# Attention's exponentials kept in the scores' bank, with a written beginning and a turned end, in a two-layer hybrid encoder

## The chip, the cores and the metric

The kernel runs on one core of one Trainium2 chip. The metric is the device time of one execution in microseconds (us), the median of several runs. The engines are called by the profile's names: PE is TensorE (matmuls; PEld its weight loads), DVE is VectorE, ACT is ScalarE, POOL is GpSimd, SP is SyncE, which issues most transfers. A bank is one of the eight parts of PSUM, 512 fp32 columns wide, which matmuls write. GpSimd does not use banks in this kernel.

## The reference

Everything is fp32; 512 tokens of 1024 channels go through two layers, each with an MLP behind it:

```python
for i in range(2):
    h = rms_norm(x, g[0])
    m = parallel_conv_mla(h, ...) if i == 0 else conformer_conv(h, ...)
    x = x + rms_norm(m, g[1])
    x = x + rms_norm(squared_relu_mlp(rms_norm(x, g[2])), g[3])

def parallel_conv_mla(h, ...):             # layer 0
    gate_b, gate_c, xs, q_lat, kv_lat, k_rope = split(h @ w_in)
    y_a = gate_b * depthwise_conv(gate_c * xs, width 3)
    q = (rms_norm(q_lat) @ w_uq) per head; k_nope, v = (rms_norm(kv_lat) @ w_ukv) per head
    y_b = softmax((q . k) * scale) @ v     # 8 heads, rotary part of 32, 512 x 512 scores
    return concatenate([y_a, y_b]) @ w_out

def conformer_conv(h, ...):                # layer 1
    u = a * sigmoid(g)                     # a, g = split(h @ w_pw1 + b)
    u = silu(layer_norm(depthwise_conv(u, width 31) + b))
    return u @ w_pw2 + b

def squared_relu_mlp(h, w1, w2):           # hidden 4096
    return square(relu(h @ w1)) @ w2
```

## The kernel before

Channels lie on the 128 partitions, tokens on the free axis: x is eight tiles of 128 x 512. Each fp32 product is made of three matmuls on values split into a high and a low part (`mm`, lines 246 to 248: high by high, high by low, low by high). A weight strip of 128 x 1024 is loaded by SP, rounded to its high part by ACT (L223), and its low part is subtracted by POOL (L224); two raw buffers and eight pairs of split ones turn over. `accum` hands out banks: three named S, two pj; one more is named o and two mi.

The order of work. Most instructions are put in order by a planner that simulates the engines; inside a `manual_schedule` the named engines keep the order in which the code writes them. `strip` calls come from a queue that `take` keeps some strips ahead.

- *Beginning* (L554 to L618). x comes in eight tiles; DVE scales each by a gain (L572), ACT rounds it (L230), DVE subtracts the low part (L233). The squares of x are summed (`Sum`, L358 and L333), summed over channels by matmuls (L368), `rstd` (L384) finds the root on DVE, `spread` (L433) brings it to all partitions, and R0 is 1 over the root mean square. The projections of the raw x (`linear` with win's strips) are multiplied by R0 afterwards (L608), so their banks are held until R0 is there. Five strips make the latents, the sixth the rotary key, twelve the short convolution.
- *Attention* (`project`, `attend`, in the order of `ATT`). For each head and block of 128 queries: scores into a bank S (L759), maximum (L761), exponential with its sum from the bank into an SBUF tile pr (L764), reciprocal, scaling of pr in place (L767; on POOL for head 7's first three blocks, else on DVE), transposes into a bank mi (L770), split into the pair PT (ACT L230, DVE L236), and after two blocks the product with V into o.
- *Two halves and a program.* After attention the tokens are cut into halves A and B. `M2` is a list of steps: up and down are the MLP's two products, pw1 and pw2 the conformer's, norm, join and finish the chains of small steps between. While a chain runs, `hold` and `pace` pull following steps of the other half to fill TensorE (`step` stops at a step of the same half). The depthwise convolution runs on DVE in pieces: `fill` adds a credit in us for each step of TensorE's, and taps are issued as long as the credit pays for them (0.395 us each with two convolutions under way, 0.525 alone). Half A is 272 wide in layer 0, B 240; in layer 1 both are 256.
- *End* (`turn`, `end`). For half B the last product is turned, tokens on partitions. `end_step` adds the last group (L1029), squares (L1031), multiplies by the gain on POOL (L1032), makes the root (L1035 with `rstd`), scales and adds the residual (L1051) and stores (L1055). Its second block's second half of columns goes in two pieces.

Of the kernel before, what the change touches and what calls it, by code (L numbers as in the profile page):

```python
# [9 lines left out]
F32 = mybir.dt.float32  # L10
# [22 lines left out]
PAD = 16  # L33
M0 = [('wout', 'A'), ('join', 'A', 0, 1), ('wout', 'B')]
M1 = []
M2 = [('up', 'A', 0, 0, 0, 8), ('join', 'B', 0, 1), ('down', 'A', 0, 0, 0, 8), ('up', 'A', 0, 1, 0, 8), ('down', 'A', 0, 1, 0, 8), ('up', 'A', 0, 2, 0, 8), ('down', 'A', 0, 2, 0, 8), ('up', 'A', 0, 3, 0, 8), ('down', 'A', 0, 3, 0, 8), ('join', 'A', 0, 3), ('up', 'B', 0, 0, 0, 8), ('down', 'B', 0, 0, 0, 4), ('pw1', 'A', 0, 8), ('down', 'B', 0, 0, 4, 8), ('up', 'B', 0, 1, 0, 8), ('down', 'B', 0, 1, 0, 8), ('up', 'B', 0, 2, 0, 2), ('norm', 'A'), ('up', 'B', 0, 2, 2, 8), ('down', 'B', 0, 2, 0, 8), ('pw2', 'A', 0, 8), ('join', 'A', 1, 1), ('up', 'B', 0, 3, 0, 8), ('down', 'B', 0, 3, 0, 8), ('join', 'B', 0, 3), ('up', 'A', 1, 0, 0, 8), ('down', 'A', 1, 0, 0, 4), ('pw1', 'B', 0, 8), ('down', 'A', 1, 0, 4, 8), ('up', 'A', 1, 1, 0, 8), ('down', 'A', 1, 1, 0, 8), ('up', 'A', 1, 2, 0, 6), ('norm', 'B'), ('up', 'A', 1, 2, 6, 8), ('down', 'A', 1, 2, 0, 8), ('up', 'A', 1, 3, 0, 4), ('pw2', 'B', 0, 8), ('join', 'B', 1, 1), ('up', 'A', 1, 3, 4, 8), ('down', 'A', 1, 3, 0, 8), ('up', 'B', 1, 0, 0, 8), ('turn', 'B', 1, 0, 0, 6), ('finish', 'A'), ('turn', 'B', 1, 0, 6, 8), ('up', 'B', 1, 1, 0, 8), ('residual', 'B'), ('turn', 'B', 1, 1, 0, 8), ('up', 'B', 1, 2, 0, 8), ('turn', 'B', 1, 2, 0, 8), ('up', 'B', 1, 3, 0, 8), ('end', 'B', 1, 3)]
# [6 lines left out]
START = ['x', (128,), 'x', (256, 512, 768), 'x', 'x', 'x', 'x', 'x', 'x', ()]  # L43
ADD0 = 0
LAG = 4
MULT_POOL = (0, 0, 0, 0, 0, 0, 0, 3)
W0 = True
WHOLE = (True,) * 5
WL = True
# [81 lines left out]
def trunk(ctx: ExitStack, tc: tile.TileContext, a, out: bass.AP, out_b: bass.AP):  # L131
# [435 lines left out]
    s0 = Sum(NC, FULL, nc.gpsimd if ADD0 else nc.vector, whole=W0)

    def split_x(j):
        load_x(xs[j], j)  # L570
        t, (hi, lo) = scratch(T), (h.t[:, :T] for h in hs[j])
        nc.vector.tensor_scalar(out=t, in0=xs[j].t, scalar1=col(gains(0, 0) + j), scalar2=None, op0=ALU.mult)  # L572
        settle()
        split((hi, lo), t, nc.vector, late=late)
        if j >= LAG:
            s0.square(xs[j - LAG].t)

    win, j = [], 0
    for what in START:
        if what == "x":  # L580
            split_x(j)
            j += 1
        else:
            win.append(strip(a["win"][len(win)], cuts=what))
    nc.sync.dma_start(kst, a["consts"])
    nc.sync.dma_start(vec[:, V_QN:], a["vecs"][:, V_QN:])
    settle()
    for j in range(NC - LAG, NC):
        s0.square(xs[j].t)
        settle()  # L590
# [299 lines left out]
    def up_step(tok, h, layer, g, m):  # L890
# [124 lines left out]
    def end_step(tok, h, layer, g):  # L1015
# [19 lines left out]
        def root(b):  # L1035
            s = misc()[:, :1]
            p = parts[b]
            if len(p) == 3:
                nc.vector.scalar_tensor_tensor(
                    out=s, in0=p[0], scalar=p[1], in1=p[2], op0=ALU.add, op1=ALU.add  # L1040
                )
            else:
                nc.vector.tensor_tensor(out=s, in0=p[0], in1=p[1], op=ALU.add)
            return rstd(s, D, tuple(f[:, b : b + 1] for f in f12))

        def leave(b, r, n):
            w = T // n
            for f in range(2):
                for i in range(n):
                    m, x = (t[:, i * w : i * w + w] for t in turned[b, f][1:])  # L1050
                    nc.vector.scalar_tensor_tensor(  # L1051
                        out=x, in0=m, scalar=r, in1=x, op0=ALU.mult, op1=ALU.add
                    )
                    q = nc.scalar if i % 2 else nc.sync
                    q.dma_start(out_b[b * P : (b + 1) * P, f * T + i * w : f * T + i * w + w], x)  # L1055
# [204 lines left out]
```

## Time and profile before

| | |
|---|---|
| median of 3 runs | 1172.47 us (1171.79 to 1172.93) |
| profiled execution | 1173.47 us |
| its span, first to last instruction | 1171.7 us |
| busy: PE, DVE, ACT, POOL | 1134.6, 649.2, 661.5, 846.0 us |
| mean granted clock of TensorE | 0.993 |

The profile is one execution. An engine's idle time counts only where that engine sets the pace. A busy PE is not PE at its peak, because ends of pipelined matmuls are modelled; the number of matmuls in a stretch tells more. In a row, "[1.47 <-DVE ...]" is idle time before it and who ended it.

### The profile page before, as it was taken

Reading aid. Unit: us, or ns where it says so; the run is one execution under the profiler, and the core shown is the slowest. Engines: PE = TensorE matmul, PEld = TensorE weight load, DVE = VectorE, ACT = ScalarE, POOL = GpSimd, SP = SyncE. Lnnn points to the kernel's source line nnn. Section 1 sums busy time; section 2 is a strip of 40 time slices with the busy share of each in tenths; the row PEclk is TensorE's granted clock in tenths of the full one; section 3 lists DMA queues with packets and bytes.
Section 4 is the critical chain, followed back from the end, with each engine's and each line's share of the span. In section 5 each row is a group of like instructions: output and inputs, shape, how many; then the busy total and the mean of one; then the engine's idle time right before and its main releaser. Section 6 shows DMA issues by size and latency. Waiting matters only on the chain.

```text
span 1171.7 us, 22121 instructions
## 1 busy us (share of the span) xinstructions
PE 1134.6 (97%) x8492; PEld 1081.3 (92%) x8492; DVE 649.2 (55%) x1693; ACT 661.5 (56%) x1211; POOL 846.0 (72%) x408
## 2 busy tenths in 40 slices
PE   7999989999999999999999999999999999999996
PEld 5778778999999999999999999999999999898895
DVE  5672699455432222669996364589995254131134
ACT  5431677456744445744655686745566776455451
POOL 5663563148878778688898578789787878779881
PEclk9999999999999999999999899999999999999999
DMA  6421332027545555545565355556555545565530
GB/s 222 154 90 30 106 100 72 1 92 235 201 161 182 178 180 169 174 163 181 180 216 187 122 196 181 179 171 207 169 195 178 180 163 180 165 231 182 179 108 36
DMA packets 55257, 184.47 MB, mean 157 GB/s; under 512 B 6384, under 2 KB 10352, under 8 KB 55152
## 3 DMA queue, kind: packets, MB, share of 16 engines
q1 hardware_dynamic: 54576, 182.02, 46.9%
q8 instruction: 66, 1.08, 0.4%
q10 hardware_dynamic: 576, 1.05, 0.3%
q14 instruction: 39, 0.32, 0.1%
HBM read 180.94 MB, written 2.10 MB: 156 GB/s over the span
## 4 chain that ended last, share of the span: by engine, by line
PE 85%; DVE 6%; ACT 3%; DMA 3%; POOL 1%; issue 1%; SPq 0%; DVEq 0%; ACTq 0%; POOLq 0%
PE S L246 20%; PE S L247 19%; PE S L248 19%; PE pj L246 5%; PE pj L247 5%; PE pj L248 5%; PE pj L990 4%; PE S L990 4%; DMA raw<-in_win 2%; POOL wlo L224 1%; ACT whi L223 1%; DVE pr L767 1%; DMA raw<-in_w 1%; PE mi L433 1%; PE mi L770 1%
## 5 line engine op out<-in xcount | busy, mean ns | idle before, releaser
L224 POOL TENSOR_TENSOR wlo<-raw,whi 128x1024 fp32r<-128x1024 f32 (+2 forms) x347 | 802.0, 2327 | 263.2 <-ACT whi L223 243.6
L223 ACT ACTIVATE whi<-raw 128x1024 fp32r<-128x1024 f32 (+2 forms) x347 | 356.6, 1033 | 368.7 <-PE S L247 173.3
L246 PE MATMUL S<-h,whi 128*128 128x256 f32 (+3 forms) x1208 | 347.7, 291 | 5.0 <-ACT h L230 2.9
L247 PE MATMUL S<-h,whi 128*128 128x256 f32 (+3 forms) x1208 | 349.0, 290 | 0.0
L248 PE MATMUL S<-h,wlo 128*128 128x256 f32 (+3 forms) x1208 | 348.7, 289 | 0.0
L246 PEld LDWEIGHTS S<-h,whi 128*128 128x128 f32 x1208 | 229.0, 191 | 10.1 <-ACT h L230 3.4
L247 PEld LDWEIGHTS S<-h,whi 128*128 128x128 f32 x1208 | 230.5, 191 | 3.5 <-issue 0.2
L248 PEld LDWEIGHTS S<-h,wlo 128*128 128x128 f32 x1208 | 230.5, 191 | 3.3 <-POOL wlo L224 0.3
L832 DVE SCALAR_TENSOR_TENSOR pj<-u,taps,pj 128x256 f32<-128x256 f32 x464 | 192.6, 484 | 1.3
L246 PE MATMUL S<-hid,whi 128*128 128x256 f32 (+2 forms) x664 | 185.3, 281 | 1.4 <-DVE acc L333 1.2
L248 PE MATMUL S<-hid,wlo 128*128 128x256 f32 (+2 forms) x664 | 186.5, 282 | 0.0
L247 PE MATMUL S<-hid,whi 128*128 128x256 f32 (+2 forms) x664 | 186.3, 281 | 0.0
L246 PEld LDWEIGHTS S<-hid,whi 128*128 128x128 f32 x664 | 124.8, 189 | 2.5 <-DVE acc L333 1.8
L248 PEld LDWEIGHTS S<-hid,wlo 128*128 128x128 f32 x664 | 125.3, 189 | 0.0
L247 PEld LDWEIGHTS S<-hid,whi 128*128 128x128 f32 x664 | 125.3, 189 | 0.0
L246 PE MATMUL pj<-h,whi 128*128 128x256 f32 (+3 forms) x344 | 105.5, 307 | 9.5 <-ACT h L230 7.6
L248 PE MATMUL pj<-h,wlo 128*128 128x256 f32 (+3 forms) x344 | 105.3, 306 | 0.3 <-POOL wlo L224 0.3
L247 PE MATMUL pj<-h,whi 128*128 128x256 f32 (+3 forms) x344 | 105.3, 306 | 0.0
L246 PEld LDWEIGHTS pj<-h,whi 128*128 128x128 f32 x344 | 65.5, 191 | 12.4 <-ACT h L230 7.6
L236 DVE TENSOR_TENSOR hid<-S,hid 128x256 fp32r<-128x256 f32 (+2 forms) x102 | 42.9, 420 | 52.7 <-ACT hid L230 52.2
L247 PEld LDWEIGHTS pj<-h,whi 128*128 128x128 f32 x344 | 65.5, 190 | 3.4 <-DVE h L233 1.1
L248 PEld LDWEIGHTS pj<-h,wlo 128*128 128x128 f32 x344 | 65.6, 191 | 3.1 <-POOL wlo L224 0.7
(267 smaller groups left out, 1740.2 us busy)
## 6 DMA issues: line engine op xcount, KB each, us to landing
raw<-in_w SPq DMA_DIRECT2D x224, 512.0 KB, 3.3
raw<-in_pw SPq DMA_DIRECT2D x48, 512.0 KB, 3.3
raw<-in_w2t SPq DMA_DIRECT2D x32, 512.0 KB, 3.3
raw<-in_win SPq DMA_DIRECT2D x16, 512.0 KB, 3.3
x<-in_xT SPq DMA_DIRECT2D x16, 256.0 KB, 4.4
raw<-in_wout SPq DMA_DIRECT2D x8, 512.0 KB, 3.3
raw<-in_wq SPq DMA_DIRECT2D x8, 192.0 KB, 2.4
out<-x SPq DMA_DIRECT2D x8, 128.0 KB, 3.5
```

Source lines behind the costliest of these rows:

```text
L223: nc.scalar.activation(h, r, AF.Copy)
L224: nc.gpsimd.tensor_tensor(out=lo[:, c0:c1], in0=r, in1=h.bitcast(F32), op=ALU.subtract)
L236: eng.tensor_tensor(out=lo, in0=src, in1=hi.bitcast(F32), op=ALU.subtract)
L246: nc.tensor.matmul(acc, sh, mh, start=i == 0, stop=False)
L247: nc.tensor.matmul(acc, sh, ml, start=False, stop=False)
L248: nc.tensor.matmul(acc, sl, mh, start=False, stop=i == n - 1)
L433: nc.tensor.matmul(o[:, sl], r[:, b : b + 1].to_broadcast([bw, P]), ident[:bw, :bw], start=True, stop=True,)
L767: eng.tensor_scalar(out=pr_, in0=pr_, scalar1=sm, scalar2=None, op0=ALU.mult)
L770: nc.tensor.transpose(tp[:, kb * P : (kb + 1) * P], pr_[:, kb * P : (kb + 1) * P], ident)
L832: nc.vector.scalar_tensor_tensor(out=dst, in0=src, scalar=wk, in1=acc, op0=ALU.mult, op1=ALU.add)
L990: nc.tensor.matmul(acc, x, w, start=start, stop=stop)
```

## The change

Five edits go together.

1. The beginning is written out for PE, DVE and ACT. PE starts with twelve matmuls on a zeroed tile (`busy`) and does ten more after the first product. The first two strips take each x as it comes (`bit`), strips 3 and 4 follow; the sums of squares and the root stand between them. Banks of the first four products are pj, S, pj, S.
2. Attention: on 23 of the 32 blocks the exponential is written back into the bank S, and DVE scales from there into pr. On nine blocks (head 1 to 5: block 1; heads 6 and 7: blocks 0 and 2) it goes to pr and POOL scales it.
3. M2: norm A comes two up steps later, and pw2 A two up steps of the next group later.
4. The credits of up and down steps are scaled by the half's width over 256.
5. The end: the gain product is made by DVE into the bank, squares go to bank o, the last piece has a bank of its own, the mean and the first sums are made ahead, and the root is a shorter chain. The gain's load moves from ACT's queue, where it stood behind M0, to SP at the first turn step.

```diff
-... ('up', 'B', 0, 2, 0, 2), ('norm', 'A'), ('up', 'B', 0, 2, 2, 8), ('down', 'B', 0, 2, 0, 8), ('pw2', 'A', 0, 8), ('join', 'A', 1, 1), ('up', 'B', 0, 3, 0, 8), ...
+... ('up', 'B', 0, 2, 0, 4), ('norm', 'A'), ('up', 'B', 0, 2, 4, 8), ('down', 'B', 0, 2, 0, 8), ('up', 'B', 0, 3, 0, 2), ('pw2', 'A', 0, 8), ('join', 'A', 1, 1), ('up', 'B', 0, 3, 2, 8), ...
...
-MULT_POOL = (0, 0, 0, 0, 0, 0, 0, 3)
+MULT_POOL = [(h, 1) for h in range(1, 6)] + [(h, b) for h in (6, 7) for b in (0, 2)]
...
+    E = mybir.EngineType
+    with tc.manual_schedule(engines={E.PE, E.DVE, E.Activation}):
+        idle, bank = tmp("tq", F32R), ps("S")
+        nc.vector.memset(idle.bitcast(F32), 0.0)
+        def busy(n):
+            for _ in range(n):
+                nc.tensor.matmul(bank, idle[:, :P], idle, start=True, stop=True)
+        accs = []
+        def bit(i, k):
+            if len(accs) == i:
+                accs.append(ps(("pj", "S")[i % 2]))
+            (wh, wl), (xh, xl), kk = win[i], hs[k], slice(k * P, k * P + P)
+            x_h, x_l = xh.t[:, :T], xl.t[:, :T]
+            nc.tensor.matmul(accs[i], wh[:, kk], x_h, start=k == 0, stop=False)
+            nc.tensor.matmul(accs[i], wl[:, kk], x_h, start=False, stop=False)
+            nc.tensor.matmul(accs[i], wh[:, kk], x_l, start=False, stop=k == NC - 1)
+        busy(12)
+        win, scaled, sq = [], [], {}
+        total = ps("o")
+        def scale_x(j):
+            load_x(xs[j], j)
+            t = misc()
+            nc.vector.tensor_scalar(out=t, in0=xs[j].t, scalar1=col(gains(0, 0) + j), scalar2=None, op0=ALU.mult)
+            nc.scalar.activation(hs[j][0].t[:, :T], t, AF.Copy)
+            scaled.append(t)
+        def rest_x(j):
+            hi, lo = (h.t[:, :T] for h in hs[j])
+            nc.vector.tensor_tensor(out=lo, in0=scaled[j], in1=hi.bitcast(F32), op=ALU.subtract)
+        def square_x(j):
+            sq[j] = tmp("ycat") if j else total
+            nc.scalar.activation(sq[j], xs[j].t, AF.Square)
+        def add_x(j):
+            dst = tmp("ycat") if j == NC - 1 else total
+            nc.vector.tensor_tensor(out=dst, in0=total, in1=sq[j], op=ALU.add)
+            return dst
+        scale_x(0)
+        win.append(strip(a["win"][0], cuts=(128,)))
+        rest_x(0)
+        bit(0, 0)
+        busy(10)
+        scale_x(1)
+        win.append(strip(a["win"][1], cuts=(256, 512, 768)))
+        bit(1, 0)
+        for j in range(2, NC + 1):
+            if j < NC:
+                scale_x(j)
+            if j >= 5:
+                square_x(j - 5)
+            rest_x(j - 1)
+            bit(0, j - 1)
+            bit(1, j - 1)
+        win.append(strip(a["win"][2]))
+        nc.sync.dma_start(kst, a["consts"])
+        nc.sync.dma_start(vec[:, V_QN:], a["vecs"][:, V_QN:])
+        for j in range(1, NC):
+            if j + 3 < NC:
+                square_x(j + 3)
+            if j == 4:
+                win.append(strip(a["win"][3]))
+            last = add_x(j)
+        for k in range(NC):
+            bit(2, k)
+        win.append(strip(a["win"][4]))
+        s0 = Sum(NC, FULL)
+        s0.parts = [last]
+        root = rstd(s0.done(STARTS), D, inverse=inv0)[:, :NB]
+        for k in range(NC - 2):
+            bit(3, k)
+        nc.scalar.activation(R0, spread(root), AF.Copy)
+        for k in range(NC - 2, NC):
+            bit(3, k)
+    scope["turn"] = 3
...
-            acc = linear(win[m0 + j] if m0 + j < len(win) else strip(a["win"][m0 + j]), hs)
+            acc = accs[m0 + j] if m0 + j < len(accs) else linear(win[m0 + j], hs)
...
-            nc.scalar.activation(pr_, S, AF.Exp, bias=mx, scale=SCALE, accum_out=sm)
+            on_pool = (h, b) in MULT_POOL
+            e = pr_ if on_pool else S
+            nc.scalar.activation(e, S, AF.Exp, bias=mx, scale=SCALE, accum_out=sm)
             nc.vector.reciprocal(sm, sm)
-            eng = nc.gpsimd if b < MULT_POOL[h] else nc.vector
-            eng.tensor_scalar(out=pr_, in0=pr_, scalar1=sm, scalar2=None, op0=ALU.mult)
+            eng = nc.gpsimd if on_pool else nc.vector
+            eng.tensor_scalar(out=pr_, in0=e, scalar1=sm, scalar2=None, op0=ALU.mult)
...
-        fill(FILL["up"])
+        fill(FILL["up"] * seg.w / 256)
-        fill(FILL["sum" if last else "down" if g else "first"])
+        fill(FILL["sum" if last else "down" if g else "first"] * seg_of(h, layer).w / 256)
...
-            turned["gain"] = gtok
+            nc.sync.dma_start(gtok, a["gain"].to_broadcast([P, D]))
...
+        scaled = {b: [] for b in range(2)}
+        def piece(b, f, cols, acc=None):
+            bank, m, x = turned[b, f]
+            acc = bank[:, cols] if acc is None else acc
+            m, x, g = m[:, cols], x[:, cols], gtok[:, f * T + cols.start : f * T + cols.stop]
             nc.vector.tensor_tensor(out=m, in0=acc, in1=m, op=ALU.add)
             sm = small(1)
+            nc.scalar.activation(ps("o")[:, : acc.shape[-1]], m, AF.Square, accum_out=sm)
+            nc.vector.tensor_tensor(out=acc, in0=m, in1=g, op=ALU.mult)
             parts[b].append(sm)
+            scaled[b].append((acc, x, f * T + cols.start))
+        def near(b):
+            fd, v = small(1), small(1)
+            nc.vector.tensor_scalar(
+                out=fd, in0=f12[1][:, b : b + 1], scalar1=1.0 / D, scalar2=None, op0=ALU.mult
+            )
+            v0 = parts[b][0]
+            for p in parts[b][1:]:
+                nc.vector.tensor_tensor(out=v0, in0=v0, in1=p, op=ALU.add)
+            nc.vector.tensor_scalar(out=v, in0=v0, scalar1=fd, scalar2=EPS, op0=ALU.mult, op1=ALU.add)
+            return fd, v
+        def root(b, fd, v):
+            nc.vector.scalar_tensor_tensor(
+                out=v, in0=parts[b][-1], scalar=fd, in1=v, op0=ALU.mult, op1=ALU.add
+            )
+            r, y, q, out = (small(1) for _ in range(4))
+            nc.vector.tensor_scalar(
+                out=r.bitcast(I32), in0=v.bitcast(I32), scalar1=-0.5, scalar2=float(0x5F3759DF),
+                op0=ALU.mult, op1=ALU.add,
+            )
+            nc.vector.scalar_tensor_tensor(out=y, in0=r, scalar=v, in1=r, op0=ALU.mult, op1=ALU.mult)
+            nc.vector.tensor_scalar(out=q, in0=y, scalar1=0.375, scalar2=-1.25, op0=ALU.mult, op1=ALU.add)
+            nc.vector.tensor_scalar(out=q, in0=q, scalar1=y, scalar2=1.875, op0=ALU.mult, op1=ALU.add)
+            nc.vector.tensor_tensor(out=r, in0=q, in1=r, op=ALU.mult)
+            nc.vector.scalar_tensor_tensor(out=y, in0=r, scalar=v, in1=r, op0=ALU.mult, op1=ALU.mult)
+            nc.vector.tensor_scalar(out=q, in0=y, scalar1=-0.5, scalar2=1.5, op0=ALU.mult, op1=ALU.add)
+            nc.vector.scalar_tensor_tensor(
+                out=out, in0=q, scalar=r, in1=f12[0][:, b : b + 1], op0=ALU.mult, op1=ALU.mult
+            )
+            return out
+        def leave(b, r):
+            for i, (m, x, c) in enumerate(scaled[b]):
+                nc.vector.scalar_tensor_tensor(out=x, in0=m, scalar=r, in1=x, op0=ALU.mult, op1=ALU.add)
+                q = nc.scalar if i % 2 else nc.sync
+                q.dma_start(out_b[b * P : (b + 1) * P, c : c + x.shape[-1]], x)
+        def rest(f, cols, acc=None):
+            acc = turned[1, f][0][:, cols] if acc is None else acc
+            n = f * T + cols.start
             for k in range(NC):
+                issue([turn_mm(acc, h, ws[k], k, 1, slice(0, cols.stop - cols.start), n)])
         for f in range(2):
             piece(0, f, slice(0, T))
+            if f == 0:
+                fd, v = near(0)
         rest(0, slice(0, T))
+        leave(0, root(0, fd, v))
         piece(1, 0, slice(0, T))
         for i in range(2):
             cols = slice(i * T // 2, (i + 1) * T // 2)
+            acc = (ps("S") if i else turned[1, 1][0])[:, : T // 2]
+            rest(1, cols, acc)
+            if i:
+                fd, v = near(1)
+            piece(1, 1, cols, acc)
+        leave(1, root(1, fd, v))
...
-    nc.scalar.dma_start(gtok, a["gain"].to_broadcast([P, D]))
```

## Rows read from the trace of the kernel before

**Rows 1.** The page: busy time of each engine.
```profile
PE 1134.6 (97%) x8492; PEld 1081.3 (92%) x8492; DVE 649.2 (55%) x1693; ACT 661.5 (56%) x1211; POOL 846.0 (72%) x408
```

**Rows 2.** TensorE's waits, whole span: waiter, releaser, total us, times, longest.
```profile
PE o L247 <- DVE s L762: 2.5, 3, 1.3
...
PE pj L990 <- ACT pj L1031: 1.1, 1, 1.1
...
PE S L246 <- ACT pr L764: 0.5, 1, 0.5
...
PE mi L662 <- DVE ycat L660: 0.3, 1, 0.3
```

**Rows 3.** Windows: length, busy us (x instructions), granted clock, DMA share, GB/s.
```profile
7.60:12.40 4.80, 4.79 (x10) 3.11 (x11) 3.85 (x6) 3.78 (x8) 3.93 (x4) 1.00 1.01 353
12.40:17.20 4.80, 4.80 (x22) 3.86 (x21) 4.70 (x9) 3.90 (x7) 0.96 (x2) 1.00 0.82 296
...
140.00:200.00 60.00, 55.05 (x351) 47.67 (x350) 58.23 (x130) 44.75 (x96) 33.08 (x19) 1.00 0.30 101
200.00:216.00 16.00, 15.79 (x117) 14.57 (x116) 12.54 (x36) 10.60 (x26) 4.67 (x3) 1.00 0.01 2
...
648.60:654.20 5.60, 5.60 (x28) 5.60 (x28) 4.32 (x12) 4.60 (x12) 0.00 (x0) 0.50 0.00 0
654.40:660.00 5.60, 5.60 (x49) 5.60 (x48) 0.00 (x0) 3.18 (x6) 2.04 (x1) 1.00 0.00 0
```

**Rows 4.** Timeline of the beginning: start, us, engine, line, operation, count.
```profile
0.73 0.42 ACTq L1133 DMA_DIRECT2D gtok<-in_gain  x1
...
7.61 0.80 PE L246 MATMUL pj<-h,whi 128*128 128x512 f32 x1 [7.61 <-ACT h L230]
...
11.56 0.63 PE L248 MATMUL S<-h,wlo 128*128 128x512 f32 x1
...
23.04 1.06 ACT L223 ACTIVATE whi<-raw 128x1024 fp32r<-128x1024 f32 x1 [1.04 <-DMA raw<-in_win]
...
24.18 2.40 POOL L224 TENSOR_TENSOR wlo<-raw,whi 128x1024 fp32r<-128x1024 f32 x1 [1.98 <-ACT whi L223]
...
42.04 0.50 PE L246 MATMUL pj<-h,whi 128*128 128x512 f32 x1 [1.47 <-DVE ycat L608]
...
57.22 0.69 DVE L630 TENSOR_SCALAR ycat<-mi 128x512 f32<-128x512 f32 x1
```

**Rows 5.** Attention, by line: duration ns min/median/max, first and last start.
```profile
L767 DVE TENSOR_SCALAR pr<-pr,s x29: 469/486/3669, 138.4 to 215.8; 128x512 f32<-128x512 f32 x29
...
L767 POOL TENSOR_SCALAR pr<-pr,s x3: 1563/1563/1572, 208.0 to 211.9; 128x512 f32<-128x512 f32 x3
...
L236 DVE TENSOR_TENSOR pt<-mi,pt x32: 661/680/693, 142.9 to 225.2; 128x512 fp32r<-128x512 f32 x32
...
L761 DVE TENSOR_REDUCE s<-S x32: 669/678/692, 135.5 to 210.1; 128x1 f32<-128x512 f32 x32
...
L764 ACT ACTIVATE pr<-S,s x32: 667/688/692, 137.4 to 214.8; 128x512 f32<-128x512 f32 x32
```

**Rows 6.** TensorE's waits from 630 to 660 us, around norm A.
```profile
PE mi L433 <- DVE s L419: 2.3, 1, 2.3
PE S L246 <- ACT h L230: 1.9, 1, 1.9
PE mi L368 <- DVE acc L333: 0.5, 1, 0.5
```

**Rows 7.** Timeline of the end.
```profile
1162.30 0.28 PE L990 MATMUL pj<-whi,hid 128*128 128x256 f32 x1
...
1163.14 0.39 ACT L1031 ACTIVATE pj<-u 128x256 f32<-128x256 f32 x1 [3.75 <-DVE u L1029]
...
1163.68 0.79 DVE L1039 SCALAR_TENSOR_TENSOR mi<-s,s,s 128x1 f32<-128x1 f32 x1 [0.58 <-ACT pj L1031]
...
1167.22 1.67 DVE L1051 SCALAR_TENSOR_TENSOR u<-u,s,u 128x256 f32<-128x256 f32 x4
```

More of the change, by code (lines that the diff above doesn't have):

```diff
@@ L35 @@
 M1 = []
-M2 = [('up', 'A', 0, 0, 0, 8), ('join', 'B', 0, 1), ('down', 'A', 0, 0, 0, 8), ('up', 'A', 0, 1, 0, 8), ('down', 'A', 0, 1, 0, 8), ('up', 'A', 0, 2, 0, 8), ('down', 'A', 0, 2, 0, 8), ('up', 'A', 0, 3, 0, 8), ('down', 'A', 0, 3, 0, 8), ('join', 'A', 0, 3), ('up', 'B', 0, 0, 0, 8), ('down', 'B', 0, 0, 0, 4), ('pw1', 'A', 0, 8), ('down', 'B', 0, 0, 4, 8), ('up', 'B', 0, 1, 0, 8), ('down', 'B', 0, 1, 0, 8), ('up', 'B', 0, 2, 0, 2), ('norm', 'A'), ('up', 'B', 0, 2, 2, 8), ('down', 'B', 0, 2, 0, 8), ('pw2', 'A', 0, 8), ('join', 'A', 1, 1), ('up', 'B', 0, 3, 0, 8), ('down', 'B', 0, 3, 0, 8), ('join', 'B', 0, 3), ('up', 'A', 1, 0, 0, 8), ('down', 'A', 1, 0, 0, 4), ('pw1', 'B', 0, 8), ('down', 'A', 1, 0, 4, 8), ('up', 'A', 1, 1, 0, 8), ('down', 'A', 1, 1, 0, 8), ('up', 'A', 1, 2, 0, 6), ('norm', 'B'), ('up', 'A', 1, 2, 6, 8), ('down', 'A', 1, 2, 0, 8), ('up', 'A', 1, 3, 0, 4), ('pw2', 'B', 0, 8), ('join', 'B', 1, 1), ('up', 'A', 1, 3, 4, 8), ('down', 'A', 1, 3, 0, 8), ('up', 'B', 1, 0, 0, 8), ('turn', 'B', 1, 0, 0, 6), ('finish', 'A'), ('turn', 'B', 1, 0, 6, 8), ('up', 'B', 1, 1, 0, 8), ('residual', 'B'), ('turn', 'B', 1, 1, 0, 8), ('up', 'B', 1, 2, 0, 8), ('turn', 'B', 1, 2, 0, 8), ('up', 'B', 1, 3, 0, 8), ('end', 'B', 1, 3)]
@@ new lines @@
+M2 = [('up', 'A', 0, 0, 0, 8), ('join', 'B', 0, 1), ('down', 'A', 0, 0, 0, 8), ('up', 'A', 0, 1, 0, 8), ('down', 'A', 0, 1, 0, 8), ('up', 'A', 0, 2, 0, 8), ('down', 'A', 0, 2, 0, 8), ('up', 'A', 0, 3, 0, 8), ('down', 'A', 0, 3, 0, 8), ('join', 'A', 0, 3), ('up', 'B', 0, 0, 0, 8), ('down', 'B', 0, 0, 0, 4), ('pw1', 'A', 0, 8), ('down', 'B', 0, 0, 4, 8), ('up', 'B', 0, 1, 0, 8), ('down', 'B', 0, 1, 0, 8), ('up', 'B', 0, 2, 0, 4), ('norm', 'A'), ('up', 'B', 0, 2, 4, 8), ('down', 'B', 0, 2, 0, 8), ('up', 'B', 0, 3, 0, 2), ('pw2', 'A', 0, 8), ('join', 'A', 1, 1), ('up', 'B', 0, 3, 2, 8), ('down', 'B', 0, 3, 0, 8), ('join', 'B', 0, 3), ('up', 'A', 1, 0, 0, 8), ('down', 'A', 1, 0, 0, 4), ('pw1', 'B', 0, 8), ('down', 'A', 1, 0, 4, 8), ('up', 'A', 1, 1, 0, 8), ('down', 'A', 1, 1, 0, 8), ('up', 'A', 1, 2, 0, 6), ('norm', 'B'), ('up', 'A', 1, 2, 6, 8), ('down', 'A', 1, 2, 0, 8), ('up', 'A', 1, 3, 0, 4), ('pw2', 'B', 0, 8), ('join', 'B', 1, 1), ('up', 'A', 1, 3, 4, 8), ('down', 'A', 1, 3, 0, 8), ('up', 'B', 1, 0, 0, 8), ('turn', 'B', 1, 0, 0, 6), ('finish', 'A'), ('turn', 'B', 1, 0, 6, 8), ('up', 'B', 1, 1, 0, 8), ('residual', 'B'), ('turn', 'B', 1, 1, 0, 8), ('up', 'B', 1, 2, 0, 8), ('turn', 'B', 1, 2, 0, 8), ('up', 'B', 1, 3, 0, 8), ('end', 'B', 1, 3)]
@@ L42 @@
 FILL = {'up': 2.3, 'down': 2.3, 'first': 2.6, 'sum': 1.8, 'pw1': 4.8, 'pw2': 2.3}
-START = ['x', (128,), 'x', (256, 512, 768), 'x', 'x', 'x', 'x', 'x', 'x', ()]
-ADD0 = 0
-LAG = 4
-MULT_POOL = (0, 0, 0, 0, 0, 0, 0, 3)
+MULT_POOL = [(h, 1) for h in range(1, 6)] + [(h, b) for h in (6, 7) for b in (0, 2)]
 W0 = True
@@ L565, in trunk @@
     hs = [hpair() for _ in range(NC)]
[L567 to L590, printed above, removed]
     def spread_sb(r):
@@ L599, in trunk @@
     inv0 = cp.tile([P, len(STARTS)], F32, name="inv0")
-    nc.scalar.activation(R0, spread(rstd(s0.done(STARTS), D, inverse=inv0)[:, :NB]), AF.Copy)
+    E = mybir.EngineType
[69 more added lines that the diff above has]
+            bit(3, k)
@@ L1024, in end_step @@
         parts = {b: [] for b in range(2)}
-        def piece(b, f, cols):
-            acc, m, _ = turned[b, f]
-            acc, m, g = acc[:, cols], m[:, cols], turned["gain"][:, f * T + cols.start : f * T + cols.stop]
+        scaled = {b: [] for b in range(2)}
[3 more added lines that the diff above has]
+            m, x, g = m[:, cols], x[:, cols], gtok[:, f * T + cols.start : f * T + cols.stop]
             nc.vector.tensor_tensor(out=m, in0=acc, in1=m, op=ALU.add)
@@ L1030, in piece @@
             sm = small(1)
-            nc.scalar.activation(acc, m, AF.Square, accum_out=sm)
-            nc.gpsimd.tensor_tensor(out=m, in0=m, in1=g, op=ALU.mult)
+            nc.scalar.activation(ps("o")[:, : acc.shape[-1]], m, AF.Square, accum_out=sm)
+            nc.vector.tensor_tensor(out=acc, in0=m, in1=g, op=ALU.mult)
             parts[b].append(sm)
[L1035 to L1055, printed above, removed]
@@ L1057, in rest @@
-        def rest(f, cols):
+            scaled[b].append((acc, x, f * T + cols.start))
[9 more added lines that the diff above has]
+            return fd, v
@@ L1058, in rest @@
+        def leave(b, r):
[6 more added lines that the diff above has]
+            n = f * T + cols.start
             for k in range(NC):
-                issue([turn_mm(turned[1, f][0], h, ws[k], k, 1, cols, f * T)])
+                issue([turn_mm(acc, h, ws[k], k, 1, slice(0, cols.stop - cols.start), n)])
@@ L1061, in end_step @@
         for f in range(2):
             piece(0, f, slice(0, T))
+            if f == 0:
+                fd, v = near(0)
         rest(0, slice(0, T))
-        r = root(0)
-        leave(0, r, 1)
+        leave(0, root(0, fd, v))
         piece(1, 0, slice(0, T))
@@ L1068, in end_step @@
             cols = slice(i * T // 2, (i + 1) * T // 2)
-            rest(1, cols)
-            piece(1, 1, cols)
-        leave(1, root(1), 2)
+            acc = (ps("S") if i else turned[1, 1][0])[:, : T // 2]
[4 more added lines that the diff above has]
+        leave(1, root(1, fd, v))
     def run(program, in_order=True):
```

## The prediction

> **What bounds the kernel now.** I read the page first: of a span of 1171.7 us the matmuls fill 1134.6 [rows 1]. So TensorE sets the time, and a change can only win where TensorE waits, runs at the lower clock, or has not begun or has already ended. The table of TensorE's waits says where that is, and the timeline around each place says why. There are four places, and this change touches all four.
>
> *Beginning.* The first matmul starts at 7.61. Up to 12.4 ten matmuls of 512 columns take 4.8 us, then 22 take the same time [rows 3, 4]. The granted clock is shown as 1.00 for both, but 0.48 against 0.22 us is the 1.2 GHz level against the 2.4 GHz level; the engine had done nothing before. At 42.04 TensorE waits 1.47 us because all five score and projection banks hold products that wait for R0 [rows 4].
>
> *Attention.* From 140 to 200 us VectorE is busy 58.2 of 60 us and TensorE is idle 4.95 [rows 3]; the waits named are for VectorE [rows 2]. The reader should see one odd row: the 29 scalings on VectorE have a median of 486 ns and a maximum of 3669 ns [rows 5]. I laid the long ones (eight of the 29) beside GpSimd's instructions: each overlaps one of GpSimd's subtractions and ends when it ends. The 29 take 24.1 us in all, 14.1 at the median, so 10.0 us of VectorE is waiting. The scaling reads and writes SBUF. VectorE's low-part subtraction reads a bank, ran 32 times in the same stretch, and never left 661 to 693 ns [rows 5].
>
> *Norm A.* TensorE waits 0.5, 2.3 and 1.9 us at three steps of the layer norm [rows 6], and just after the granted clock is 0.50, the 1.2 GHz level: 28 matmuls in 5.6 us, against 49 later [rows 3]. That cost 2.4 us, and 0.2 more in the half microsecond before.
>
> *End.* TensorE waits 1.1 us for a square that is written into its bank [rows 2]; after its last matmul, through at 1162.6 [rows 7], 9.1 us follow.
>
> **The change part by part.**
>
> *Beginning.* Taken away: the lower level (11 matmuls at 0.43, 2.4 us), since 12 idle matmuls run from about 1.4 us; and the wait for a bank (1.47), since the root is now asked for in the middle of strip 3, some 7 us earlier. The gain vector (512 KB, issued on ScalarE's queue at 0.73 [rows 4]) no longer loads beside the first x: at the 353 GB/s of that stretch [rows 3] that is up to 1.5 us earlier, or nothing if the planner puts it first on SP. Added: waits of the written order. Two strips need 6 matmuls for each x, 1.32 us, so after the second strip's first low part (before: 11.56 [rows 4]) seven more x take 9.2 us, to 20.8. Strip 2's high part now stands on ScalarE behind the eighth x and two squares, at about 18; with 1.06 for it and 2.40 for the low part on GpSimd [rows 4] it is ready at 21.5. Then 72 matmuls (15.8), and sums and spread. Before, 42.04 - 7.61 less 120 matmuls (26.4), 2.4 and 1.47 left 4.1 for sums, spread and small waits; I keep 3.0. The sixth strip starts at 40.3 instead of 42.0: gain 1.7, between -0.5 (every wait 1 us longer) and 4 (all of 2.4 and 1.47). VectorE's backlog behind R0 starts earlier, so TensorE's wait for it at the rotary key (L662, 0.3 us [rows 2]) should go. The ten idle matmuls after the first product (2.2 us) lie in the time up to 11.56. Together 2.0.
>
> *Attention.* Removed: six of 29 scalings go to GpSimd (nine there instead of three), and the other 23 read the bank. No row has that form here; the nearest, a tensor_scalar from a bank into SBUF, took 0.69 [rows 4], so 23 x 0.69 = 15.9 us instead of 24.1. Bounds: 23 x 0.49 = 11.3 if it kept its speed, and 24.1 if it still waited for GpSimd; the low-part subtraction says it does not wait. VectorE falls by 8.2 us, about 7 of them in the stretch: from 58.2 to 51 of 60. TensorE then has the most work there (55.05 busy) and its idle 4.95 should fall to about 1: gain 4.0. Bounds: 6, if waits past 200 us go too, and -2, below. GpSimd gets six more pieces of 1.56 us [rows 5] to its 33.1 of 60 [rows 3]; around the three of before TensorE was idle for 0.2 of 16 us [rows 3]. ScalarE writes a bank instead of SBUF: 0.69 each today [rows 5], and with 44.75 of 60 busy it has room either way.
>
> Against the change speaks the price of the bank: 0.69 by the row where the scaling out of SBUF has a median of 0.49, 4.6 us more over 23. The Trainium skill says the same in "VectorE: DVE Perf Modes", "Why PSUM operands drop a tier": an operand in a bank takes fp32 down to one element a cycle. By that page's cycle table the scaling would be 0.66 us by estimate, 15.2 in all instead of 15.9, which moves no wait of TensorE.
>
> *Order of M2 and scaled credits.* In norm A each hold pulls one step of the other half as filler; 14 steps stand between norm A and pw2 A in both versions. I counted credits by the code. Before: 8 x 4.8 + 4 x 2.6 + 18 x 2.3 = 90.2 us by the norm; 256 taps cost 101 and more (a lone one 0.525), so 31 are left, four to a hold: 8 holds. Two each for mean, squares and root follow, the 14 are gone, and the third hold of the root finds none: that is the 2.3 us. After: two more steps stand ahead of the norm, each worth 240/256; 91.3, 28 taps, 7 holds, and the root gets its third filler. A filler is 24 matmuls of 240 columns, 2.7 us (24 x 5.6 / 49 [rows 3]), so the 2.3 goes. The waits of 0.5 and 1.9 stay: no filler is left for the last loop. What is late next is that 1.9. I take it that the clock then stays up, since 4.95 us of scattered idle in attention did not lower it [rows 3]; that gives 2.6. Together 4.9; 2.3 if the clock falls all the same, 9 if every wait there goes. VectorE also gets 6% less convolution per step of 240 columns; nothing waits on that.
>
> *End.* The second half of the last product gets a bank of its own: 1.1 us wait gone [rows 2]. After the last square a sum of 0.79 and 14 small operations run from 1163.68 to 1167.22 [rows 7], 3.54 in all; the 14 take 2.75, 0.196 each. Nine such are left, 1.77; the mean and the first sums are made before. Gain 1.8. The gain product moves from GpSimd to VectorE and lies beside the square (0.42, by the adds of the same form; the square begins at 1163.14 and its sum is there at 1163.68 [rows 7]). Three adds instead of four: 0.1 to 0.2. Sum 3.1, between 2.2 and 4. The gain vector's load now stands on SP in the strips' queue; transfers are 0.3 to 0.6 busy, strips are fetched ahead, so nothing; without that cover up to 1.5.
>
> **Sum.** 2.0 + 4.0 + 4.9 + 3.1 = 14.0. The profiled execution took 1173.47, 1.8 more than its span of 1171.7, which I take as unchanged: 1159.5. The median of the runs, 1172.47, lies 1.0 lower, so 1158.5.
>
> **The rivals.**
>
> *The clock falls anyway* after norm A (two waits of 2.4 us together remain): 2.6 of the gain is missing, 1161.
>
> *Attention gains nothing*, because GpSimd's nine pieces stand behind its strip subtractions of 2.4 us and TensorE waits for them instead: 1162.5. For it: GpSimd is first in first out, and from 140 to 200 it is at 33 of 60 us. Against: the three pieces from 208 to 213.5 [rows 5] lie where TensorE hardly waited [rows 3].
>
> *The score banks* (slower). A bank was free after the exponential; now for 23 blocks it is held until the scaling is over. Blocks come every (210.1 - 135.5) / 31 = 2.41 us [rows 5], so three banks allow 7.2 us each. The durations alone (matmuls 0.7, maximum 0.68, two small ones 0.3, exponential 0.69 and its sum 0.19, scaling 0.69) make 3.3; 3.9 is left for queues. TensorE has already waited 0.5 for a bank [rows 2]. The other three parts bring 10.0, so it is slower by over 2.3 only if attention loses 12.3, 0.4 a block: banks held 8.4 us, 5.1 of it queueing. VectorE's queue, the cause of most of it, gets shorter. A small loss (the -2 above) is likelier.
>
> *The scaling still waits for GpSimd* although it reads a bank: attention keeps its 24 us, the rest comes: 1162.5 too.
>
> **How the numbers follow.** The forecast has 0.50; clock falls 0.20 (1161); attention gains nothing, by either way, 0.15 (1162.5); more than forecast (norm A's waits go, beginning gains 4) 0.07 (1153). Within 0.2%, 2.3 us, about what a measurement of this kernel can tell from no change: beginning and attention each lose 2 and the clock falls, 0.05. Slower by the banks: 0.03. So faster 0.92, same 0.05, slower 0.03. The range leaves out the last two, and what lies past the bounds of beginning and attention together: 1152 (front 4, attention 5, norm 8, end 3.5) to 1166 (beginning 0, attention -1, norm 4.9, end 2.6).
>
> **What would show it.** Right: VectorE's scalings near 0.69 us with no long ones; TensorE idle about 1 us from 140 to 200; one wait at norm A fewer and no stretch at 0.50 after it; sixth strip near 40; under 7.5 us between the last matmul and the end. Wrong: waits of TensorE for a bank's release in attention, the transposes waiting for GpSimd, strip 2's low part later than 22 us, or 0.50 again near 645.

## The result and the profile after

Median 1163.89 us (1163.42 to 1165.08) against 1172.7 in the same rounds: ratio 0.9924, 95% interval 0.9908 to 0.9939. The profiled execution took 1163.42, its span is 1161.6, 10.1 less than before. The medians differ by 8.8: the profiled execution of before lies above its median, and this one is the shortest of its four. Ratios are of the fast runs alone: one execution in experiment e7, at 5506 us, was slow and is left out. By the timeline's marks (the first score matmul, the MLP's first matmul, the first turned product, the last instruction) the 10.1 lie so:

| stage | before | after | forecast | measured |
|---|---|---|---|---|
| beginning and projections, to the first scores | 131.1 | 129.4 | -2.0 | -1.7 |
| attention and output product, to the MLP | 131.7 | 128.7 | -4.0 | -2.9 |
| M2, to the first turned product | 737.3 | 734.6 | -4.9 | -2.7 |
| end | 171.7 | 168.9 | -3.1 | -2.7 |

Two of the measured numbers have two parts. Of the beginning's 1.7, 0.6 lies ahead of the sixth strip (42.0 to 41.4) and 1.1 behind it. Of attention's 2.9, 2.1 lies between the first scores and the last product with V (96.1 us before, 94.0 after) and 0.8 in the output product behind it.

TensorE's waits, whole span, after (to [rows 2]):

```profile
PE S L243 <- ACT h L227: 3.0, 2, 1.9
...
PE pj L591 <- POOL wlo L221: 1.6, 1, 1.6
...
PE mi L430 <- DVE s L416: 1.3, 1, 1.3
...
PE S L243 <- DVE pr L825: 0.3, 1, 0.3
```

No wait for a square at the end is left. The strip's low part is a new wait in the beginning. The root's wait at norm A is 1.3 where it was 2.3 [rows 6], and one wait for a bank, behind a scaling, is there.

Around norm A TensorE's timeline shows where the new filler went, before and after (L368 and L365 sum the squares, L433 and L430 spread the root):

```profile
642.15 0.58 PE L368 MATMUL mi<-kst,acc 128*128 128x1 f32 x4 [0.53 <-DVE acc L333]
645.04 1.22 PE L433 MATMUL mi<-kst,s 128*128 128x128 f32 x4 [2.32 <-DVE s L419]
```

```profile
641.33 0.50 PE L365 MATMUL mi<-kst,acc 128*128 128x1 f32 x4
...
644.14 1.06 PE L430 MATMUL mi<-kst,s 128*128 128x128 f32 x4 [1.31 <-DVE s L416]
```

Between the spread of the mean and the sum stand 94 matmuls of the other half where 67 stood; between the sum and the root's spread stand 8 where none stood.

Windows after (length, busy us of PE, PEld, DVE, ACT, POOL, granted clock, DMA share, GB/s), to [rows 3]:

```profile
138.00:198.00 60.00, 57.33 (x361) 49.14 (x360) 52.45 (x127) 45.13 (x97) 39.66 (x24) 1.00 0.30 101
...
644.40:651.20 6.80, 4.87 (x23) 4.57 (x23) 5.16 (x16) 5.90 (x16) 1.89 (x1) 0.50 0.45 152
651.20:657.00 5.80, 5.80 (x50) 5.80 (x50) 1.01 (x3) 1.82 (x4) 0.00 (x0) 1.00 0.01 3
```

In the dense part of attention TensorE's idle time fell from 4.95 to 2.67 and VectorE from 58.2 to 52.5. Behind norm A the granted clock is 0.50, the 1.2 GHz level, once more, now for 6.8 us; before it was 10.2:

```profile
644.00:654.30 10.30, 7.35 (x32) 7.06 (x33) 6.99 (x22) 6.43 (x16) 1.07 (x1) 0.50 0.27 94
```

Attention's lines after (duration ns min/median/max), to [rows 5]:

```profile
L825 DVE TENSOR_SCALAR pr<-S,s x23: 733/751/753, 136.8 to 211.4; 128x512 f32<-128x512 f32 x23
L825 POOL TENSOR_SCALAR pr<-pr,s x9: 1563/1565/1574, 144.2 to 209.6; 128x512 f32<-128x512 f32 x9
...
L822 ACT ACTIVATE S<-S,s x23: 632/662/674, 135.8 to 210.3; 128x512 f32<-128x512 f32 x23
```

No scaling is long any more, as forecast; but each takes 0.75, not 0.69.

The beginning and the end after, timelines, to [rows 4, 7]:

```profile
10.05 0.33 SPq L219 DMA_DIRECT2D raw<-in_win  x1
...
11.38 0.43 SPq L1030 DMA_DIRECT2D gtok<-in_gain  x1
...
12.82 10.43 SPq L219 DMA_DIRECT2D raw<-in_win  x2
...
19.39 1.05 ACT L220 ACTIVATE whi<-raw 128x1024 fp32r<-128x1024 f32 x1
...
20.51 2.38 POOL L221 TENSOR_TENSOR wlo<-raw,whi 128x1024 fp32r<-128x1024 f32 x1 [7.72 <-ACT whi L220]
...
22.94 0.50 PE L591 MATMUL pj<-h,wlo 128*128 128x512 f32 x1 [1.58 <-POOL wlo L221]
...
41.44 0.39 PE L243 MATMUL pj<-h,whi 128*128 128x512 f32 x1
...
1153.66 0.28 PE L1048 MATMUL S<-whi,hid 128*128 128x256 f32 x1
...
1155.04 0.22 DVE L1110 SCALAR_TENSOR_TENSOR s<-s,s,s 128x1 f32<-128x1 f32 x1 [0.17 <-ACT o L1091]
...
1157.06 0.75 DVE L1131 SCALAR_TENSOR_TENSOR u<-S,s,u 128x512 f32<-128x512 f32 x1
```

The planner put the gain's load on SP at 11.38, behind the third strip's (10.05) and ahead of the fourth's (12.82). TensorE waits 1.58 us for the third strip's low part. ScalarE rounds that strip at 19.39 without waiting for its transfer, which landed at 14.7. The sixth strip starts at 41.4. At the end 7.7 us follow the last matmul where it was 9.1.

### The profile page after: what moved, and what is told of

Read it like the earlier page. It is cut to its first block, busy times and chain, and to the rows that moved or that the text cites. A ratio compares the mean times of both kernels' runs of the same rounds, so it can differ in the third digit from the quotient of the medians.

```text
span 1161.6 us, 22196 instructions
## 1 busy us (share of the span) xinstructions
PE 1137.3 (98%) x8514; PEld 1084.6 (93%) x8514; DVE 644.6 (55%) x1684; ACT 661.7 (57%) x1212; POOL 849.5 (73%) x409
## 4 chain that ended last, share of the span: by engine, by line
PE 92%; ACT 2%; DMA 2%; DVE 2%; issue 1%; POOL 1%; SPq 0%; DVEq 0%; ACTq 0%; POOLq 0%
PE S L243 21%; PE S L244 21%; PE S L245 21%; PE pj L243 5%; PE pj L244 5%; PE pj L245 5%; PE S L1048 4%; PE pj L1048 4%; POOL wlo L221 1%; PE mi L828 1%; DMA raw<-in_win 1%; PE mi L365 1%; ACT whi L220 1%; PE mi L430 1%; PE o L244 1%
## 5 line engine op out<-in xcount | busy, mean ns | idle before, releaser
L243 PE MATMUL S<-h,whi 128*128 128x256 f32 (+3 forms) x1200 | 343.7, 290 | 4.9 <-ACT h L227 3.0
L244 PE MATMUL S<-h,whi 128*128 128x256 f32 (+3 forms) x1200 | 345.6, 289 | 0.0
L243 PE MATMUL S<-hid,whi 128*128 128x256 f32 (+2 forms) x672 | 187.8, 281 | 2.0 <-DVE acc L330 2.0
L244 PE MATMUL S<-hid,whi 128*128 128x256 f32 (+2 forms) x672 | 188.6, 281 | 0.0
L243 PEld LDWEIGHTS S<-hid,whi 128*128 128x128 f32 x672 | 126.5, 189 | 3.0 <-DVE acc L330 2.6
L244 PEld LDWEIGHTS S<-hid,whi 128*128 128x128 f32 x672 | 126.8, 189 | 0.0
L243 PE MATMUL pj<-h,whi 128*128 128x256 f32 (+3 forms) x320 | 95.6, 299 | 0.3 <-DVE h L230 0.3
L244 PE MATMUL pj<-h,whi 128*128 128x256 f32 (+3 forms) x320 | 95.7, 299 | 0.0
L245 PE MATMUL pj<-h,wlo 128*128 128x256 f32 (+3 forms) x320 | 95.5, 298 | 0.0
L243 PEld LDWEIGHTS pj<-h,whi 128*128 128x128 f32 x320 | 60.9, 190 | 2.1 <-DVE h L230 0.6
L245 PEld LDWEIGHTS pj<-h,wlo 128*128 128x128 f32 x320 | 60.9, 190 | 1.8 <-issue 0.2
L244 PEld LDWEIGHTS pj<-h,whi 128*128 128x128 f32 x320 | 60.9, 190 | 1.8 <-issue 0.2
```

Source lines behind the costliest of these rows:

```text
L243: nc.tensor.matmul(acc, sh, mh, start=i == 0, stop=False)
L244: nc.tensor.matmul(acc, sh, ml, start=False, stop=False)
L245: nc.tensor.matmul(acc, sl, mh, start=False, stop=i == n - 1)
```

## Experiments

Each is the changed kernel with one edit. Single spans are compared with its 1161.6, and the stages of the table above; ratios are to the kernel before, and their intervals are some 0.0015 to either side, so differences of under 3 us rest on the stages. These vary too. In the kernels whose edit leaves a stage as it is, the sixth strip starts at 40.9 to 41.7, attention takes 128.2 to 128.7 where the clock stays up, and M2 takes 734.1 to 735.5. A difference of that size shows nothing.

**Attention: the bank, or GpSimd?**

```diff
-MULT_POOL = [(h, 1) for h in range(1, 6)] + [(h, b) for h in (6, 7) for b in (0, 2)]
+MULT_POOL = [(7, b) for b in range(3)]
...
-            e = pr_ if on_pool else S
+            e = pr_
```

This is e1; e3 has the second cut alone and keeps the nine.

> The changed kernel with attention's edit undone: exponentials go to the SBUF tile, scaled there in place, three blocks on GpSimd as before. Theory (the scalings no longer wait for GpSimd's subtractions, and that is attention's gain): again several scalings of over 1.3 us on VectorE, from the first score matmul to the end of the wout products 2.9 us longer than in the changed kernel, span 1164.5. Rival (the stage was shortened by the earlier R0 and the lighter VectorE queue ahead of it): the stage stays within 0.7 us of the changed kernel's, span 1162.

> The changed kernel with nine scalings on GpSimd, but every exponential in the SBUF tile as before. Theory: 23 scalings have a median of 0.49 us again and some wait for GpSimd up to 2.4 us or more; about 6 us of such waits, VectorE as busy as in the changed kernel but in lumps, loss of 1 to 2.5, span 1163 to 1164. Rival (taking nine off VectorE is the gain, and the bank only makes the rest slower): span 1161.5 or less.

`MULT_POOL = []` with `e = S`, all 32 on VectorE out of the bank:

> The changed kernel with all 32 scalings on VectorE out of the bank, none on GpSimd. Theory (the bank does it): VectorE has 9 x 0.75 = 6.8 us more, about 58 of 60 busy in the dense stretch, so half of the 2.9 us is lost, span 1163. Rival (the nine on GpSimd do it): the whole 2.9 or more is lost, span 1164.5 or over.

e11 has sixteen:

```diff
-MULT_POOL = [(h, 1) for h in range(1, 6)] + [(h, b) for h in (6, 7) for b in (0, 2)]
+MULT_POOL = [(h, b) for h in range(8) for b in (0, 2)]
```

> The changed kernel with sixteen scalings on GpSimd (blocks 0 and 2 of every head) instead of nine. Theory (taking scalings off VectorE is what pays in attention, and TensorE's idle 2.7 us of the dense stretch still waits for VectorE): VectorE 5 us less busy, stage 1 us shorter, span 1160.6. Rival (GpSimd, first in first out behind its strip subtractions, is late for the transposes): stage 1 us or more longer.

| | bank | on GpSimd | attention stage | span | ratio |
|---|---|---|---|---|---|
| e1 | no | 3 | 130.8 | 1164.3 | 0.9933 |
| e2 | yes | 0 | 130.0 | 1163.5 | 0.9931 |
| e3 | no | 9 | 129.1 | 1161.3 | 0.9924 |
| changed kernel | yes | 9 | 128.7 | 1161.6 | 0.9924 |
| e11 | yes | 16 | 129.1 | 1162.8 | 0.9923 |

The scalings of e1, then of e3:

```profile
L825 DVE TENSOR_SCALAR pr<-pr,s x29: 469/486/3676, 136.7 to 214.3; 128x512 f32<-128x512 f32 x29
```

```profile
L825 DVE TENSOR_SCALAR pr<-pr,s x23: 469/487/2148, 136.2 to 212.0; 128x512 f32<-128x512 f32 x23
```

The edit is worth 2.1 us (e1). Nine pieces on GpSimd without the bank bring 1.7 of it (130.8 to 129.1). The 0.4 that the bank then adds is no more than the stage varies by, so beside the nine no gain of the bank is shown; the bank alone, with no piece on GpSimd, brings 0.8 (e2). In e3 single scalings again take up to 2.1 us, yet its 23 take 17.6 us together, against 17.2 out of the bank (23 x 0.75). What the bank saves in waits it costs in speed. The rival of e3 was nearer than the theory. Of the waits in e2 the longest sum is one that the changed kernel has once:

```profile
PE S L243 <- DVE pr L825: 2.7, 7, 0.7
```

TensorE waits for score banks that a scaling still holds. Sixteen on GpSimd leave VectorE idle (48.0 of 60 busy) and gain nothing: the same wait is 1.7 us, and the output product starts 3 us later. That theory fell, and the rival's loss of 1 us did not come either.

**Norm A: order, credits, fillers.** e4 takes M2 and the credits of before; e12 only the credits; e5 moves pw2 A two more up steps:

```diff
-... ('up', 'B', 0, 3, 0, 2), ('pw2', 'A', 0, 8), ('join', 'A', 1, 1), ('up', 'B', 0, 3, 2, 8), ...
+... ('up', 'B', 0, 3, 0, 4), ('pw2', 'A', 0, 8), ('join', 'A', 1, 1), ('up', 'B', 0, 3, 4, 8), ...
```

> The changed kernel with M2's order and the unscaled credits of before. Theory (one filler more at norm A covers its wait for the root and shortens the stretch at the lower clock): the root's wait is 2.3 again, 10.2 us at 0.50 instead of 6.8, span 2.7 longer, 1164.3. Rival (the clock's stretch is not tied to the fillers): only the wait comes back, 1.5 longer, span 1163.1.

> The changed kernel with pw2 A another two up steps later: 16 steps between norm A and pw2 A instead of 14. Theory (what is left at norm A is a lack of filler, and the clock falls because of it): the waits of 1.3 and 1.9 us go but for 0.5, no stretch at 0.50, span 4 to 5 shorter, 1157. Rival A (the clock falls whatever fills): 2.7 shorter, 1159. Rival B (VectorE and ScalarE have no room for two more up steps in the chain, so the chain ends later): under 1 shorter.

> The changed kernel with M2's new order but credits as before, not scaled by the width. Theory (by the count of holds the convolution then needs six instead of seven, and one filler is left for norm A's last loop): the wait for the root is gone and the wait of 1.9 us shrinks by about 1, span 1 to 2.5 shorter, the more if the clock stays up. Rival (VectorE, given 6% more convolution a step, falls behind and ends the chain later): as long or longer.

TensorE's waits around norm A in e4, e5 and e12:

```profile
PE mi L430 <- DVE s L416: 2.3, 1, 2.3
PE S L243 <- ACT h L227: 1.9, 1, 1.9
PE mi L365 <- DVE acc L330: 0.5, 1, 0.5
```

```profile
PE S L243 <- ACT h L227: 0.7, 2, 0.4
```

```profile
PE S L243 <- ACT h L227: 2.9, 1, 2.9
```

The M2 stage: e4 736.6, changed kernel 734.6, e12 732.4, e5 731.1 (spans 1162.6, 1161.6, 1159.5, 1157.9; ratios 0.9934, 0.9924, 0.9900, 0.9883). The waits of before return in e4, as the theory says. Its stretch at 0.50 is 6.8 us in the traced execution, as in the changed kernel, and not the 10.2 of before. But the instructions there do not set the length of that stretch alone: in e3, e6 and e7, whose norm A is the changed kernel's, it is 3.4 us. So this trace can't say what the fillers do to it.

In e5 two more fillers take away 2.5 us of the 3.2 us of waits, the clock shows 1.00 through the norm, and the stage is 3.5 us shorter; the mean granted clock is 0.998 in all four executions. In e12 the wait for the root is gone, as expected, but the wait of 1.9, which was to shrink by about 1, is 2.9. That is nearly what the changed kernel waits, in one piece, and in the traced execution the clock stayed:

```profile
640.00:660.00 20.00, 17.07 (x142) 16.72 (x142) 8.36 (x28) 15.61 (x33) 10.52 (x6) 1.00 0.34 119
```

Its gain of 2.2 is then nearly the clock's alone. The mean granted clock of e12's four executions is 0.999, 0.997, 0.999 and 0.997, with spans of 1159.5, 1160.2, 1158.8 and 1160.0, so in two of them it was down for longer, at a place that no trace shows. All four spans lie under the four of the changed kernel (1161.6 to 1163.3): scaling the credits by the width, one of the five edits, cost about 2 us here.

**Beginning: the third strip, the gain, the idle matmuls.**

```diff
             if j < NC:
                 scale_x(j)
+            if j == NC - 1:
+                win.append(strip(a["win"][2]))
...
-        win.append(strip(a["win"][2]))
```

> The changed kernel with the third strip rounded on ScalarE before the last x's squares instead of after four of them. Theory (TensorE's 1.6 us wait at 21.4 us is the written order on ScalarE): the wait goes, the sixth strip starts 1.5 us earlier, at 39.9, and the span is 1.5 shorter, 1160.1. Rival (the strip's transfer, issued at 12.8 behind the gain, or GpSimd's queue is as late): the wait keeps more than 1 us, span 1161.5.

e8 issues the gain on ScalarE's queue behind M0, as before; e10 leaves out `busy(12)` and `busy(10)`:

> The changed kernel with the gain's load on ScalarE's queue, where it stood before. Theory (x comes later behind 512 KB, but the third strip, whose transfer then no longer stands behind the gain, sets the sixth strip's start): first x 2 us later, sixth strip within 0.7 us of the changed kernel's 41.4, span within 0.8 of 1161.6. Rival (the beginning is bound by x's arrival): sixth strip and span 1.5 to 2 us later.

> The changed kernel without its 22 idle matmuls at the start. Theory (the first 11 or so products run at the lower level, 2.4 us, but TensorE then waits 1.6 us less for the third strip's low part, which does not hang on it): sixth strip 0.8 later, 42.2, span 0.8 longer. Rival (the whole 2.4 us shows): sixth strip 43.8.

The waits of e6 in the first 70 us:

```profile
PE pj L591 <- POOL wlo L221: 0.7, 1, 0.7
```

e6: the sixth strip starts at 40.1 instead of 41.4, the span is 1159.7, the ratio 0.9909: the written order on ScalarE was most of that wait. The theory of e8 and the rival of e6 take the third strip's transfer to stand behind the gain; the timeline has it ahead (10.05 and 11.38). e8: 42.2, span 1164.7 (ratio 0.9935). e10: 42.0, span 1164.1 (0.9939). In both the sixth strip comes 0.5 to 0.8 later, near what the theories say, though that is little more than its start varies by. The traced spans lose 2.5 to 3.0, more than the 0.8 expected. Of that, 1.1 to 1.4 lies in attention, where the clock falls for 3.4 us and had stayed up in the changed kernel, and 0.7 to 0.9 in M2, which is what M2 varies by. Windows of e8, from the start and from attention:

```profile
9.40:12.80 3.40, 3.40 (x10) 2.63 (x9) 2.00 (x4) 2.42 (x6) 3.40 (x4) 0.50 1.01 348
```

```profile
169.80:173.20 3.40, 3.40 (x18) 3.40 (x17) 3.26 (x9) 2.10 (x5) 2.18 (x2) 0.50 0.32 127
```

e10 has the same stretch at 169.9 to 173.2. Their attention stages are 130.1 and 129.9; the changed kernel's instructions are the same there, in the same order on TensorE. That these two edits bring the falls is not shown: e8's four executions have mean clocks from 0.992 to 0.995 and spans from 1164.7 (the traced one) to 1162.2, and the last lies among the changed kernel's.

**End.** The old `piece`, `root`, `leave` and `rest`:

> The changed kernel with the end of before (square into its own bank, gain product on GpSimd, long root). Theory: TensorE waits 1.1 us again before its last product and 9.1 us follow its last matmul, span 2.7 longer, 1164.3. Rival (the end's time is set by the last transfers): under 1 longer.

End stage 171.6 against 168.9, span 1163.7, ratio 0.9948; the wait before the last product is back:

```profile
PE pj L1048 <- ACT pj L1089: 1.1, 1, 1.1
```

**Both finds together**, e5's order and e6's strip:

> The changed kernel with both: two more fillers at norm A, and the third strip rounded before the last squares. Theory (the two places don't touch): the gains add, 3.7 + 1.9 = 5.6, span 1156.0. Rival (where TensorE's clock falls depends on more than the fillers, and it falls again in attention or at norm A): 1157.5 or more.

Median 1158.7 (1158.15 to 1159.03), ratio 0.9875 (0.9859 to 0.9892), span 1157.2: 4.5 less than the changed kernel where 5.6 was expected. The clock fell neither in attention nor at norm A. The sixth strip came at 40.3 and the low part's wait was 0.7 as in e6; the stages add to within 1.1. It beats both kernels. Over e5 alone (ratio 0.9883) the 0.0008 is inside the intervals, so what e6's strip adds to e5's order is seen in the first scores' start (128.3 against 129.4), not in the time.

## Why the prediction was right, and where it was too large

The forecast of 1158.5 was 5.4 below the measured 1163.9, which lies in the range. The side and all four places were right; all four terms were too large, the beginning's and attention's by more than the stages show. Of the signs named for being right, few came: no long scalings, and one wait fewer at norm A. Three of those for being wrong came: a wait for a bank in attention, though of 0.3 us only, strip 2's low part later than 22 us, and 0.50 again near 645. The range held because each place still gave part of its term.

*Beginning* (2.0, measured 1.7). That the numbers agree is partly luck: the sixth strip came 0.6 earlier, not 1.7, and the time behind it was 1.1 shorter where 0.3 was forecast. The mechanism was right: x came earlier (first scaling at 4.1 instead of 6.2, and at 6.7 in e8, which has the gain's load where it was), the bank wait went, the low part of strip 2 (the third strip) became the wait. It came at 22.9, not 21.5, because ScalarE began the strip at 19.4 and not at about 18; its transfer had landed at 14.7, so the gain's load did not hold it up. e6 shows it: with the strip earlier on ScalarE the wait fell from 1.6 to 0.7. Behind the sixth strip, the 30 matmuls around the rotary key took 6.3 us instead of 7.3: the wait there went, as forecast, but the gain was 1.0 and not 0.3. No run undoes the written beginning as a whole.

*Attention* (4.0, measured 2.9, of which the edit is 2.1 by e1). The other 0.8 was not forecast: it lies in the output product, where a wait of TensorE for VectorE's sum (0.6 before) is gone in every kernel with the new beginning, e1 too. No run tells why. The step that failed is "23 x 0.69 = 15.9 us instead of 24.1". The waits went as said, but the scaling took 0.75, so 17.2; and e3 reaches 17.6 without the bank. "No row has that form here" was an oversight: the trace of before has a tensor_scalar out of a bank with a scalar for each partition, at 0.74 us:

```profile
64.40 0.74 DVE L648 TENSOR_SCALAR x<-mi,kst 128x512 f32<-128x512 f32 x1
```

(The Trainium skill's rule that an operand in a bank costs speed, "VectorE: DVE Perf Modes", "Why PSUM operands drop a tier", agrees: 0.75 against a median of 0.49 in e3. The estimate of 0.66 from its cycle table was too short, further than the row's 0.69.) So VectorE's relief was nearly all the six scalings given to GpSimd, by the forecast's numbers the smaller part (6 x 0.49 = 2.9 of 8.2). TensorE's idle time went to 2.7, not to 1. Of the rivals, "attention gains nothing" was half wrong and half right about GpSimd: no wait of TensorE is for one of the nine pieces, and sixteen gain nothing. The score banks do bind where VectorE scales more blocks (e2), with the sign and place that the slower rival named, but at 2.7 us, far from its price.

*Norm A* (4.9, measured 2.7). The rival with a chance of 0.20 came true: "the clock falls anyway". Within the forecast the failing step is "the root gets its third filler": of the 35 matmuls more that stand in the chain, 27 came ahead of the sum, where they took its wait of 0.5, and only 8 (1.0 us) behind it, so the root's wait went from 2.3 to 1.3 and not to nothing. And "I take it that the clock then stays up" was wrong. e5 and e12 show that it can; beyond the waits that each took away, their M2 gained 1.0 and 1.9 us. Why 3.2 us of waits in two pieces let it fall, and 2.9 in one do not, these runs don't settle; part of it lies outside norm A, as the stretches of 3.4 and 6.8 us at the same instructions show.

*End* (3.1, measured 2.7). Right by e7. The part with the wait for the square gave 1.3 where 1.1 was forecast, what follows the last matmul 1.4 of 1.9: nine steps took 2.0 (1155.04 to 1157.06), 0.22 each and not 0.196, and the last three adds saved nothing.

## What to carry to other kernels

Read the minimum, median and maximum of one line before its mean: a line that stretches only beside another engine's work names the engine to relieve. But cost both cures by all the instructions they change: here moving work off VectorE paid, and moving its operand to a slower place gave back as price what it saved in waits. Where one engine is 97% busy, count the fillers of each chain against the holds that ask for one; two more steps moved in a list (e5, 3.5 us of its stage) were worth more than attention's edit (2.1). And look at more than one execution before you explain a fall of the clock.

## What the runs showed of the hardware

- A scaling with a scalar for each partition out of a bank took 0.75 us (an addition of that form before, L648, 0.74), where one with constants took 0.69 [rows 4]; the exponential into its own bank took 0.66, into SBUF 0.69.
- TensorE's granted clock fell to 0.50 for 10.2 us at norm A before, 6.8 after, 3.4 in e3, e6 and e7 with the same instructions there, and not at all in e5, e9 and e12. In attention it fell for 3.4 in e8 and e10, whose first scores come 0.6 to 0.7 us later, and in no other trace. Executions of one kernel differ as well: e12's mean clock is 0.999 or 0.997. What decides was not settled. The Trainium skill ("TensorE: Matmul & The Clock Gate", "What's actually happening") has the clock follow a watch on activity that runs freely, not begun with the kernel; that a shift alone changes the outcome would fit it, but no run here varied the start alone.
- Scalings that read and wrote SBUF were stretched beside GpSimd again, to 3.68 us in e1 and 2.15 in e3, and none out of a bank was (the changed kernel, e2, e11: 0.76 at most).
